# One encoder step: prompt attention with one subtracted map and one transpose, sample keys with four heads to a tile, and a pool of their own for the V rows

## The chip, the cores and the metric

The kernel runs on one core of a Trainium2 chip. The metric is the time of one launch in microseconds (us) on the device. Before the change it is 2169.43 us, the median of three runs (2169.18 to 2169.60).

## The reference, cut to what matters

One layer for 512 prompt tokens (one sequence) and 8 x 16 sample tokens (eight sequences, each with 1024 cached keys and values). Each of four attention heads makes two softmax maps and subtracts the second, times lam, from the first:

```python
def diff_core(q, k, v, qpos, kpos, lam):
    s = jnp.einsum('bqhmd,bkhmd->bhmqk', q, k, preferred_element_type=jnp.float32) * (B_DK ** -0.5)
    ...
    p = jax.nn.softmax(s, axis=-1)
    a = p[:, :, 0] - lam * p[:, :, 1]
    return jnp.einsum('bhqk,bkhd->bqhd', a.astype(v.dtype), v)

def run_group(x, c, past_k, past_v, ...):
    h = layer_norm(x) * (1 + scale1) + shift1
    p = h @ w_in[l]          # spatial gating, attention and gated DeltaNet read their columns
    ...
    y = jnp.concatenate([ya, yb, yc], axis=-1) @ w_out[l]
    x = layer_norm(DN_ALPHA * x + gate1 * y, ln1_g[l], ln1_b[l])
    h2 = layer_norm(x) * (1 + scale2) + shift2
    f = peer(h2, ...)        # 8 heads x top 16 of 16384 experts for each token
    x = layer_norm(DN_ALPHA * x + gate2 * f, ln2_g[l], ln2_b[l])

def peer_block(h, w_query, sub_keys, expert_u, expert_v):
    ...                      # ids (n, 128) and gates (n, 128) from two top-16 lists
    act = jax.nn.gelu(jnp.einsum('nkd,nd->nk', expert_u[ids], h))
    return jnp.einsum('nk,nkd->nd', (gates * act).astype(h.dtype), expert_v[ids])
```

## The kernel before

**The stages.** In order of time: the modulation and the combined projection; the attention stage, in which the prompt's attention, the samples' attention and the gated DeltaNet run side by side; the output projection; the choice of experts; the table; and the last stage, which works through all 16384 experts in 128 blocks of 128.

**The attention stage.** `lanes` (L127) writes four generators into one program: two chains of DeltaNet tiles (`gdn`), the prompt's attention (`attn_prompt` for the query tiles t = 0 to 3) and the samples' (`attn_sample`). A scheduler in the framework then orders the instructions of each engine at build time, and on the chip each engine runs its list in that order. `attn_prompt` takes a head at a time: two score products into PSUM, an addition of the mask with a row maximum on VectorE (DVE, L785), two exponentials on ScalarE (ACT, L789). The softmax's row factors and lam are then put on the diagonals of two 128x128 matrices `dg` (L794), and for each block of 128 keys two matrix products (s of map 0 by `dg` 0, plus s of map 1 by `dg` 1) give the transposed difference in PSUM: scaling, subtraction and transpose in one. `aT` (L801) is its copy, and a product with V follows. The DeltaNet ends before the prompt's lane; heads 1 to 3 of t = 3 stand alone behind it.

`attn_sample` takes one sequence b at a time. `fetch_k` loads its keys as eight tiles `ck` of one head and 512 positions (L1086, 256 KB, six buffers), `fetch_v` its values as four tiles `cv` (two buffers). `scores` multiplies: each head's product fills 32 of the 128 columns of TensorE (PE) and 32 rows of one PSUM bank, so that four heads make a bank of 512 positions. All loads are issued by SyncE (SP), whose queue is also in a fixed order.

**The table.** `table` (L1562) writes the gates into a dense table `gdense` in DRAM, expert by token: 12 chunks of four steps. A step makes one-hot tiles `ob`, `o1`, `o2` on DVE (L1585, L1588, L1589) and `o1a` on ACT, and PE multiplies them into PSUM (`sa`); ACT copies the result into `stg`, and each full `stg` (two buffers) is stored to `gdense` (L1596). The pool `tp` holds all of these; `o1`, `o1a` and `o2` have three buffers each.

**The last stage.** When `tx` closes, the pool `ep` takes over the table's memory. Each block m: load of 128 rows of U (`ur`) and of V (`vr`), split of each into a high and a low part (`uh`, `ul`, `vh`, `vl`), the table's columns (`gt`, one load for four blocks) times the activations of the block (`ga`, split into `wh`, `wl`), and products on PE. Eight blocks of activations have been made ahead (`LEAD`). Beside that GpSimd (POOL) gathers, row by row, the experts of the last prompt tile and of the samples (L1636), and DVE multiplies each gathered tile (L1645, L1651); the first of these multiplications needs `h2q`. This stage is written in the order in which it runs (`manual_schedule`).

Of the kernel before, what the change touches and what calls it, by code (L numbers as in the profile page):

```python
# [169 lines left out]
def body(tc, I, O):  # L170
# [4 lines left out]
    def T(pool, shape, tag, dt=F32, **kw):  # L175
        uid[0] += 1
        return pool.tile(list(shape), dt, tag=tag, name=f"{tag}_{uid[0]}", **kw)
# [20 lines left out]
    def C(name):  # L198
        a, b = COLS[name]
        return cst[:, a:b] if a < NC_ else mask[0][:, a - NC_:b - NC_]  # L200
# [570 lines left out]
    def attn_prompt(t, L):  # L771
# [6 lines left out]
        for h in range(4):  # L778
# [12 lines left out]
            V.tensor_tensor(out=sm[:, 1:2], in0=sm[:, 1:2], in1=nlam, op=ALU.mult)  # L791
            dg = T(gp, [P, 2, P], f"dg{L}")
            for m in range(2):
                V.tensor_scalar(out=dg[:, m, :], in0=ident, scalar1=sm[:, m:m + 1], scalar2=None, op0=ALU.mult)  # L794
            yield 0.43 * (t + 1)
            pa = bank()
            for c in range(t + 1):
                for m in range(2):
                    mm(pa[:, c * P:(c + 1) * P], s[:, m, c * P:(c + 1) * P], dg[:, m, :], m == 0, m == 1)
            aT = T(gp, [P, NP], f"aT{L}")  # L800
# [275 lines left out]
    def attn_sample():  # L1076
# [5 lines left out]
        def fetch_k(b):  # L1082
            for c in range(2):
                for h in range(4):
                    ck[b, h, c] = T(sp, [P, 512], "ck", bufs=6)
                    nc.sync.dma_start(out=ck[b, h, c], in_=I["ckT"][b, h, :, c * 512:c * 512 + 512])  # L1086

# [8 lines left out]
        def scores(b):  # L1096
# [6 lines left out]
            for c, (a, e) in enumerate(((0, 512), (512, 1024), (1024, NK))):  # L1103
                ps = sbank()
                for h in range(4):
                    ql = qbd[b % 2][:, h].rearrange("p m t -> p (m t)")
                    mm(ps[32 * h:32 * h + 32, 0:e - a], ql, ck[b, h, c] if c < 2 else kTs[:, h, b * TS:(b + 1) * TS])
                V.tensor_tensor_reduce(out=s[:, a:e], in0=ps[:, 0:e - a], in1=als[:, a:e], scale=1.0, scalar=NEG,
                                       op0=ALU.add, op1=ALU.max, accum_out=mx[:, c:c + 1])
# [440 lines left out]
    def gt_load(g):  # L1550
        gts[g] = T(ep, [P, 12, 4, 32], "gt2") if g % 2 else T(rw, [P, 12, 4, 32], "gt")
        nc.sync.dma_start(out=gts[g], in_=gd_[g])

    tx = ExitStack()
    tp = pool(tx, "tp", bufs=2, side="right")

    iob8 = T(tp, [P, P, 8], "iob8", BF16, bufs=1)
    V.tensor_copy(out=iob8, in_=C("iota").unsqueeze(2).to_broadcast([P, P, 8]))

    TOGETHER = 5  # L1560

    def table():  # L1562
        for t in range(3):
# [12 lines left out]
            for c in range(4):  # L1576
                stg = T(tp, [P, P, 32], "stg")
                for n0 in range(0, 32, 8):
                    col = 32 * c + n0
                    ob = T(tp, [P, P, 8], "ob", BF16, bufs=2)  # L1580
                    m = TOGETHER
                    o1 = T(tp, [P, P, m], "o1", bufs=3)
                    o1a = T(tp, [P, 8 - m, P], "o1a", bufs=3)
                    o2 = T(tp, [P, 8, P], "o2", bufs=3)
                    V.tensor_tensor(out=ob, in0=iob8, in1=i1b[:, col:col + 8].unsqueeze(1).to_broadcast([P, P, 8]), op=ALU.is_equal)  # L1585
# [4 lines left out]
                    for q in range(0, 8, 4):  # L1590
                        pg = bank("sa")
                        for n in range(q, q + 4):
# [4 lines left out]
                                  in_=stg.rearrange("p (g i) n -> p g (i n)", g=NG))  # L1597
                if (t, c) == (2, 2):
                    gts[0] = T(rw, [P, 12, 4, 32], "gt")
                    nc.sync.dma_start(out=gts[0][:, 0:11], in_=gd_[0, :, 0:11])  # L1600
# [12 lines left out]
    gs_q = gates[:, 3, :]  # L1613
    act_s, act_q = (T(ep, [P, P], n) for n in ("act_s", "act_q"))
    h2q = T(ep, [P, D], "h2q")
    nc.sync.dma_start(out=h2q, in_=h2qd)
    facc = {3: T(ac, [P, D], "acc", bufs=4), 4: T(rw, [P, D], "ycs")}
# [34 lines left out]

    vls, vs, ws, fin, fst = {}, {}, {}, {}, {}

    def v_load(n):
        vls[n] = T(ep, [P, D], "vr", bufs=3)
        nc.sync.dma_start(out=vls[n], in_=I["v"][n * P:(n + 1) * P, :])

    def v_hi(n):
        w = vls[n]  # L1660
        if n >= NBLK - LAST:
            V.tensor_tensor(out=w, in0=w, in1=fin["p"], op=ALU.mult)  # L1662
        vs[n] = (T(ep, [P, D], "vh", F32R, bufs=LAST), T(ep, [P, D], "vl", F32R, bufs=LAST))
        S.copy(out=vs[n][0], in_=w)  # L1664
# [4 lines left out]
    def g_hi(n):  # L1669
        ga = gas[n]  # L1670
        V.tensor_tensor(out=ga.rearrange("p (c n) -> p c n", c=12), in0=ga.rearrange("p (c n) -> p c n", c=12),  # L1671
                        in1=gts[n // 4][:, :, n % 4, :], op=ALU.mult)
        ws[n] = (T(ep, [P, ND], "wh", F32R, bufs=LAST), T(ep, [P, ND], "wl", F32R, bufs=LAST))
        S.copy(out=ws[n][0], in_=ga)  # L1674
# [49 lines left out]
    def final_gates():  # L1724
        gt2 = T(ep, [P, 2, D], "gates2")
        for k, (n, sm) in enumerate((("p", "selp"), ("s", "sels"))):
            fin[n] = gt2[:, k, :]
            for hf in range(2):
                pg = bank("mm")
                mm(pg, C(sm), gm[(5, hf)])  # L1730
                S.copy(out=fin[n][:, HALF[hf]], in_=pg)
# [13 lines left out]
    obanks = iter(["sa", "tp", "sa", "tp", "sa", "so"])  # L1745
    v_load(0)
    v_load(1)
    v_hi(0)
# [7 lines left out]
    for m in range(NBLK):  # L1756
# [5 lines left out]
        if m + 2 < NBLK:  # L1762
            v_load(m + 2)
        if m % 4 == 1 and m // 4 + 1 < NG:
            gt_load(m // 4 + 1)
# [72 lines left out]
```

## Time and profile before

| what | value |
|---|---|
| median of three runs | 2169.43 us (2169.18 to 2169.60) |
| the profiled execution | 2173.13 us |
| its span | 2171.4 us |
| PE busy | 1944.2 us (90%) |
| DVE busy | 1767.7 us (81%) |
| ACT busy | 701.9 us (32%) |
| POOL busy | 806.0 us (37%) |
| moved by DMA | 572.60 MB, mean 264 GB/s |

The span runs from the first to the last instruction of the profiled execution; the execution's own time is 1.7 us longer. An engine's busy time is the time in which at least one of its instructions ran. The attention stage stands at 268 to 538 us of the span, the table at 874 to 1018, the last stage from 1018 to the end.

### The profile page before, as it was taken

What the parts mean: (1) busy time and instruction counts of PE and PEld (TensorE: products, weight loads), DVE (VectorE), ACT (ScalarE), POOL (GpSimd) and SP (SyncE); (2) the same over time, 40 slices, a digit from 0 to 9 for tenths busy, and PEclk for the clock granted to TensorE, in tenths of its full rate; (3) what the DMA queues carried; (4) which work ended last, traced back from release to release, by engine and by line L of the source; (5) the groups of instructions that cost most, each with busy time, mean ns of one, the idle gap of its engine ahead of it and who ended that gap; (6) DMA issues with size and microseconds to landing.
All of it is one profiled execution on the core that took longest, in us unless ns stands there. A gap on an engine that the chain in (4) does not pass through costs nothing.

```text
span 2171.4 us, 32392 instructions
## 1 busy us (share of the span) xinstructions
PE 1944.2 (90%) x11971; PEld 1630.7 (75%) x11971; DVE 1767.7 (81%) x3939; ACT 701.9 (32%) x1241; POOL 806.0 (37%) x637
## 2 busy tenths in 40 slices
PE   5999999997996991897999999999999999999983
PEld 3888855675565881896898888888888888888862
DVE  5752146675788999985899999999999999999987
ACT  3331222332113320786433323333333333333320
POOL 2321222110004210100466666665666666556610
PEclk8999989998997995999999999999999999999996
DMA  7354365523333210567999999999999999999961
GB/s 288 117 183 167 105 224 172 183 83 117 117 132 134 95 40 0 175 183 210 352 405 405 399 388 394 398 399 398 395 404 404 405 404 396 395 380 404 398 233 68
DMA packets 203977, 572.60 MB, mean 264 GB/s; under 512 B 20863, under 2 KB 73599, under 8 KB 198954
## 3 DMA queue, kind: packets, MB, share of 16 engines
q1 hardware_dynamic: 121994, 293.43, 37.3%
q0 software_dynamic: 73728, 268.47, 31.5%
q10 hardware_dynamic: 8096, 8.63, 1.2%
q8 instruction: 94, 1.54, 0.3%
q14 instruction: 65, 0.53, 0.1%
HBM read 535.57 MB, written 34.36 MB: 262 GB/s over the span
## 4 chain that ended last, share of the span: by engine, by line
PE 34%; DVE 20%; POOL 18%; issue 18%; DMA 6%; ACT 3%; SPq 0%; POOLq 0%; ACTq 0%; DVEq 0%
PE mm L188 15%; POOL acc L1636 9%; POOL rows L1636 9%; PE sa L188 7%; PE a L188 5%; PE g L188 3%; DVE acc L1645 2%; DVE vl L1667 1%; DVE rows L1645 1%; ACT uh L243 1%; DMA acc<-in_v_dram,ids 1%; DVE ycs L1651 1%; DMA acc<-in_u_dram,idq 1%; DVE acc L1651 1%; PE ad L188 1%
## 5 line engine op out<-in xcount | busy, mean ns | idle before, releaser
L1674 ACT CAST wh<-ga 128x384 fp32r<-128x384 f32 x128 | 65.7, 514 | 693.6 <-DVE ga L1671 693.4
L188 PE MATMUL mm<-h2h,uh 128*128 128x384 f32 x1024 | 202.8, 339 | 10.2 <-ACT uh L243 8.9
L188 PEld LDWEIGHTS mm<-h2h,uh 128*128 128x128 f32 x1024 | 178.9, 188 | 32.4 <-ACT uh L243 24.8
L188 PE MATMUL mm<-h2h,ul 128*128 128x384 f32 x1024 | 198.3, 334 | 0.0
L188 PE MATMUL mm<-h2l,uh 128*128 128x384 f32 x1024 | 198.1, 334 | 0.0
L244 DVE TENSOR_TENSOR ul<-ur,uh 128x1024 fp32r<-128x1024 f32 x127 | 155.6, 1225 | 49.5 <-ACT uh L243 49.0
L1636 POOL DMA_INDIRECT acc<-in_u_dram,idq x65 | 83.4, 1283 | 281.0 <-DVE act_q L1645 202.2
L188 PE MATMUL sa<-vh,wh 128*128 128x512 f32 x384 | 153.1, 399 | 35.9 <-ACT wh L1674 31.0
L188 PE MATMUL sa<-vl,wh 128*128 128x512 f32 x384 | 160.8, 419 | 26.8 <-DVE vl L1667 26.8
L188 PEld LDWEIGHTS mm<-h2h,ul 128*128 128x128 f32 x1024 | 179.3, 188 | 0.0
L188 PEld LDWEIGHTS mm<-h2l,uh 128*128 128x128 f32 x1024 | 179.3, 188 | 0.0
L1667 DVE TENSOR_TENSOR vl<-vr,vh 128x1024 fp32r<-128x1024 f32 x128 | 156.3, 1221 | 13.0 <-DMA vr<-in_v_dram 13.0
L188 PE MATMUL sa<-vh,wl 128*128 128x512 f32 x384 | 152.0, 396 | 0.0
L1664 ACT CAST vh<-vr 128x1024 fp32r<-128x1024 f32 x128 | 133.3, 1041 | 38.0 <-DVE vr L1662 21.4
L243 ACT CAST uh<-ur 128x1024 fp32r<-128x1024 f32 x128 | 133.9, 1047 | 15.1 <-PE mm L188 15.1
L188 PE MATMUL sa<-o,o 128*128 128x128 f32 x480 | 118.6, 408 | 12.2 <-DVE o L1589 12.2
L188 PEld LDWEIGHTS sa<-vl,wh 128*128 128x128 f32 x384 | 73.2, 191 | 65.1 <-DVE vl L1667 52.0
L188 PEld LDWEIGHTS sa<-o,o 128*128 128x128 f32 x480 | 94.8, 207 | 20.9 <-DVE o L1589 12.6
L188 PEld LDWEIGHTS sa<-vh,wh 128*128 128x128 f32 x384 | 73.0, 190 | 49.4 <-ACT wh L1674 33.5
L244 POOL TENSOR_TENSOR wlo<-raw,whi 128x2048 fp32r<-128x2048 f32 (+1 forms) x12 | 55.7, 4640 | 141.5 <-ACT whi L243 122.4
L1636 POOL DMA_INDIRECT acc<-in_v_dram,ids x65 | 84.1, 1294 | 52.1 <-DVE ycs L1651 46.9
L188 PE MATMUL tp<-vh,wh 128*128 128x512 f32 x256 | 101.6, 397 | 0.0
(472 smaller groups left out, 4762.6 us busy)
## 6 DMA issues: line engine op xcount, KB each, us to landing
ur<-in_uT_dram SPq DMA_DIRECT2D x128, 512.0 KB, 6.7
vr<-in_v_dram SPq DMA_DIRECT2D x128, 512.0 KB, 6.6
raw<-in_wada_dram SPq DMA_DIRECT2D x24, 1024.0 KB, 6.7
gdense<-stg SPq DMA_DIRECT2D x12, 2048.0 KB, 8.7
gt<-gdense SPq DMA_DIRECT2D x31, 768.0 KB, 9.3
ck<-in_ckT_dram SPq DMA_DIRECT2D x64, 256.0 KB, 4.2
cv<-in_cv_dram SPq DMA_DIRECT2D x32, 512.0 KB, 4.1
wqr<-in_wq_dram SPq DMA_DIRECT2D x32, 512.0 KB, 3.2
```

The lines of the kernel that those rows point to most:

```text
L188: PE.matmul(out, lhsT=lhsT, rhs=rhs, start=start, stop=stop, **kw)
L243: S.copy(out=hi, in_=raw)
L244: e_lo.tensor_tensor(out=lo, in0=raw, in1=hi.bitcast(F32), op=ALU.subtract)
L1636: G.indirect_dma_start(out=r, out_offset=None, in_=I["v"] if k else I["u"], in_offset=bass.IndirectOffsetOnAxis(ap=who[t][0][:, s:s + 1], ...
L1645: V.tensor_tensor_reduce(out=r, in0=r, in1=h2, scale=1.0, scalar=0.0, op0=ALU.mult, op1=ALU.add, accum_out=act[:, s:s + 1])
L1651: V.scalar_tensor_tensor(out=facc[t], in0=r, scalar=act[:, s:s + 1], in1=facc[t], op0=ALU.mult, op1=ALU.add)
L1664: S.copy(out=vs[n][0], in_=w)
L1667: V.tensor_tensor(out=vs[n][1], in0=vls.pop(n), in1=vs[n][0].bitcast(F32), op=ALU.subtract)
L1674: S.copy(out=ws[n][0], in_=ga)
```

## The change

It has three parts. In `attn_prompt` the two `dg` matrices go: ACT scales map 0 by its row factor, DVE adds map 1 times its own (which holds minus lam), both in place in `s`, and PE makes a plain transpose of each block of 128 keys. In `attn_sample` a key tile holds four heads and 256 positions (512 KB, three buffers), and each head's product covers 256 positions. For the last stage the V rows get a pool `ev`, opened ahead of the table's, their first two loads stand in the table, `o1`, `o1a` and `o2` have two buffers each, and the tiles of `ep` are allocated in another order, with the second `gt` load ahead of `h2q`.

```diff
-            dg = T(gp, [P, 2, P], f"dg{L}")
-            for m in range(2):
-                V.tensor_scalar(out=dg[:, m, :], in0=ident, scalar1=sm[:, m:m + 1], scalar2=None, op0=ALU.mult)
+
+            S.activation(s[:, 0, 0:n], s[:, 0, 0:n], AF.Copy, scale=sm[:, 0:1])
+            V.scalar_tensor_tensor(out=s[:, 0, 0:n], in0=s[:, 1, 0:n], scalar=sm[:, 1:2], in1=s[:, 0, 0:n], op0=ALU.mult, op1=ALU.add)
             yield 0.43 * (t + 1)
             pa = bank()
             for c in range(t + 1):
-                for m in range(2):
-                    mm(pa[:, c * P:(c + 1) * P], s[:, m, c * P:(c + 1) * P], dg[:, m, :], m == 0, m == 1)
+                transpose(pa[:, c * P:(c + 1) * P], s[:, 0, c * P:(c + 1) * P])
...
         def fetch_k(b):
-            for c in range(2):
-                for h in range(4):
-                    ck[b, h, c] = T(sp, [P, 512], "ck", bufs=6)
-                    nc.sync.dma_start(out=ck[b, h, c], in_=I["ckT"][b, h, :, c * 512:c * 512 + 512])
+            for c in range(4):
+                ck[b, c] = T(sp, [P, 4, 256], "ck", bufs=3)
+                nc.sync.dma_start(out=ck[b, c], in_=I["ckT"][b, :, :, c * 256:c * 256 + 256].rearrange("h d k -> d h k"))
...
-                for h in range(4):
-                    ql = qbd[b % 2][:, h].rearrange("p m t -> p (m t)")
-                    mm(ps[32 * h:32 * h + 32, 0:e - a], ql, ck[b, h, c] if c < 2 else kTs[:, h, b * TS:(b + 1) * TS])
+                for q in range(2 if c < 2 else 1):
+                    for h in range(4):
+                        ql = qbd[b % 2][:, h].rearrange("p m t -> p (m t)")
+                        if c < 2:
+                            mm(ps[32 * h:32 * h + 32, 256 * q:256 * q + 256], ql, ck[b, 2 * c + q][:, h, :])
+                        else:
+                            mm(ps[32 * h:32 * h + 32, 0:TS], ql, kTs[:, h, b * TS:(b + 1) * TS])
...
+    ev = pool(es, "ev")
     tx = ExitStack()
     tp = pool(tx, "tp", bufs=2, side="right")
...
+    vls = {}
+
+    def v_load(n):
+        vls[n] = T(ev, [P, D], "vr", bufs=3)
+        nc.sync.dma_start(out=vls[n], in_=I["v"][n * P:(n + 1) * P, :])
...
-                    o1 = T(tp, [P, P, m], "o1", bufs=3)
-                    o1a = T(tp, [P, 8 - m, P], "o1a", bufs=3)
-                    o2 = T(tp, [P, 8, P], "o2", bufs=3)
+                    o1 = T(tp, [P, P, m], "o1", bufs=2)
+                    o1a = T(tp, [P, 8 - m, P], "o1a", bufs=2)
+                    o2 = T(tp, [P, 8, P], "o2", bufs=2)
...
                 if (t, c) == (2, 2):
+                    v_load(0)
+                    v_load(1)
                     gts[0] = T(rw, [P, 12, 4, 32], "gt")
...
     act_s, act_q = (T(ep, [P, P], n) for n in ("act_s", "act_q"))
+
+    def w_pair():
+        return T(ep, [P, ND], "wh", F32R, bufs=LAST), T(ep, [P, ND], "wl", F32R, bufs=LAST)
+
+
+    first_w = w_pair()
+    first_vh = T(ep, [P, D], "vh", F32R, bufs=LAST)
     h2q = T(ep, [P, D], "h2q")
+    gates2 = T(ep, [P, 2, D], "gates2")
+    gt_load(1)
+    first_vl = T(ep, [P, D], "vl", F32R, bufs=LAST)
     nc.sync.dma_start(out=h2q, in_=h2qd)
...
-    v_load(0)
-    v_load(1)
     v_hi(0)
...
-        if m % 4 == 1 and m // 4 + 1 < NG:
+        if m % 4 == 1 and 1 < m // 4 + 1 < NG:
             gt_load(m // 4 + 1)
```

`v_hi` and `g_hi` use the first tiles for block 0, and `final_gates` uses `gates2`; nothing else is in the diff.

What the build makes of it: outside the attention stage the lists of PE, DVE, ACT and POOL hold the same instructions in the same order as before. Two places show what moved.

In PE's list of the attention stage, the key products of the sample sequence b = 3 (tiles `ck`; `cv` and `vnk` are values of b = 2, `vt` and `kT` belong to the prompt's lane, `g` to the DeltaNet), before:

```order
L188 MATMUL a_571_3620<-ck_3306,qbd_2566 32x512
L188 MATMUL a_553_3529<-cv_3269,aT_3420 32x128 x8
L188 MATMUL a_560_3589<-vt_1985,aT_556_3577 128x128 x2
L188 MATMUL a_571_3620<-ck_3308,qbd_2566 32x512
L188 MATMUL a_571_3620<-ck_3310,qbd_2566 32x512
L188 MATMUL a_571_3620<-ck_3312,qbd_2566 32x512
L188 MATMUL a_588_3666<-kT_1598,qT_2304 128x256
L188 MATMUL a_553_3529<-cv_3271,aT_3420 32x128 x8
L188 MATMUL a_553_3529<-vnk_3273,aT_3420 32x128 x4
L188 MATMUL a_572_3626<-ck_3314,qbd_2566 32x512
```

and after the change:

```order
L188 MATMUL a_550_3601<-ck_3300,qbd_2566 32x256 x4
L188 MATMUL a_550_3601<-ck_3302,qbd_2566 32x256 x4
L188 MATMUL g_567_3680<-h_498_3340,S_391_2880 64x64
L188 MATMUL a_539_3570<-vt_1985,aT_535_3558 128x128
L188 MATMUL a_532_3512<-cv_3255,aT_3404 32x128 x8
L188 MATMUL a_539_3570<-vt_1985,aT_535_3558 128x128
L188 MATMUL a_551_3611<-ck_3304,qbd_2566 32x256 x4
L188 MATMUL a_563_3647<-kT_1598,qT_2304 128x256
L188 MATMUL a_532_3512<-cv_3257,aT_3404 32x128 x8
L188 MATMUL a_532_3512<-vnk_3259,aT_3404 32x128 x4
L188 MATMUL a_564_3650<-kT_1598,qT_2304 128x256
L188 MATMUL a_551_3611<-ck_3306,qbd_2566 32x256 x4
```

Before, a sequence's first head stood alone and three heads followed together, and so in the second half. Now the four heads of a quarter follow each other; of the 32 quarters of the eight sequences six are cut into one and three.

In SP's list, from the last store of the table on, before:

```order
L1596 DMA gdense_8727<-stg_9749 128x32x128
L1616 DMA h2q_9846<-h2qd_5857 128x1024
L1657 DMA vr_9860<-in_v_dram 128x1024
L1657 DMA vr_9862<-in_v_dram 128x1024
L1497 DMA ur_9879<-in_uT_dram 128x1024
L1657 DMA vr_9881<-in_v_dram 128x1024
L1497 DMA ur_9945<-in_uT_dram 128x1024
L1657 DMA vr_9947<-in_v_dram 128x1024
L1552 DMA gt_2021_9949<-gdense_8727 128x1536
```

and after the change, first at the table's start, then from its last chunk on:

```order
L1499 DMA ur_9829<-in_uT_dram 128x1024
L1567 DMA vr_9694<-in_v_dram 128x1024
L1567 DMA vr_9696<-in_v_dram 128x1024
L1567 DMA vr_9831<-in_v_dram 128x1024
L1499 DMA ur_9895<-in_uT_dram 128x1024
L1605 DMA gdense_8671<-stg_8688 128x32x128
```

```order
L1611 DMA gt_9698<-gdense_8671 128x1408
L1605 DMA gdense_8671<-stg_9700 128x32x128
L1554 DMA gt_1947_9802<-gdense_8671 128x1536
L1637 DMA h2q_9800<-h2qd_5801 128x1024
L1567 DMA vr_9897<-in_v_dram 128x1024
L1499 DMA ur_9963<-in_uT_dram 128x1024
```

Three V tiles and two U tiles moved from behind the table's last store to ahead of its first; the second `gt` load moved ahead of `h2q`, and waits for the last store. In the built program the cast of the first V tile (`vh` of block 0) waits for the store before the last, and that of the second (`vh` of block 1) for the last, because their buffers lie over the two `stg` tiles.

## Rows read from the trace of the kernel before

**Rows 1.** Windows, all engines: stretch, us; busy us of PE, PEld, DVE, ACT, POOL; clock; DMA; GB/s

```profile
278.00:475.00 197.00, 186.87 (x2489) 123.65 (x2488) 118.23 (x456) 61.70 (x181) 37.65 (x56) 0.98 0.52 170
475.00:503.40 28.40, 25.74 (x360) 19.17 (x354) 22.66 (x100) 7.92 (x22) 2.19 (x3) 0.98 0.11 40
503.40:538.20 34.80, 23.85 (x100) 17.46 (x99) 15.18 (x64) 8.53 (x19) 0.00 (x0) 0.77 0.30 108
1010.00:1014.00 4.00, 4.00 (x22) 3.68 (x21) 1.50 (x2) 3.04 (x8) 0.00 (x0) 1.00 1.01 290
1034.00:1900.00 866.00, 839.95 (x4148) 739.52 (x4149) 818.46 (x1073) 282.13 (x405) 530.08 (x420) 1.00 1.01 396
```

**Rows 2.** Windows of tile ck alone: stretch, us; busy us of PE and PEld

```profile
278.00:475.00 197.00, 38.06 (x128) 5.30 (x128) 0.98 0.52 170
```

**Rows 3.** Windows of tile dg alone: PE, PEld and DVE

```profile
278.00:475.00 197.00, 15.49 (x96) 12.06 (x96) 7.89 (x24) 0.98 0.52 170
475.00:503.40 28.40, 2.05 (x16) 1.86 (x16) 1.11 (x4) 0.98 0.11 40
503.40:538.20 34.80, 10.54 (x48) 9.93 (x48) 0.95 (x4) 0.77 0.30 108
```

**Rows 4.** Timeline of PE: start us, duration us, line, out<-in, shape

```profile
430.47 1.04 PE L188 MATMUL a<-ck,qbd 128*32 128x512 f32 x2
445.85 1.07 PE L188 MATMUL a<-ck,qbd 128*32 128x512 f32 x8
...
553.42 1.04 PE L205 MATMUL tp<-cst,acc 128*128 128x128 f32 x8
```

**Rows 5.** Timeline of PE: work that stands between two key quarters

```profile
351.60 0.71 PE L188 MATMUL a<-vt,aT 128*128 128x128 f32 x4
353.23 0.70 PE L188 MATMUL a<-kT,qT 64*128 64x256 f32 x2
368.84 1.08 PE L188 MATMUL a<-cv,aT 128*32 128x128 f32 x32
```

**Rows 6.** Tile ck's loads, and PE's waits for them from 278 to 475

```profile
DMA to landing us min/median/max: 2.7/4.2/8.5
```

```profile
PE a L188 <- DMA ck<-in_ckT_dram: 1.5, 2, 0.9
```

**Rows 7.** Timeline: a PE transpose, ACT and DVE steps; last, the page's costliest groups

```profile
276.03 1.09 PE L205 MATMUL g<-cst,qkv 128*128 128x128 f32 x4 [1.59 <-DVE qkv L861]
482.72 0.28 DVE L794 TENSOR_SCALAR dg<-cst,sm 128x128 f32<-128x128 f32 x1
498.41 0.72 ACT L789 ACTIVATE s<-s,mx 128x512 f32<-128x512 f32 x1
```

```profile
L1667 DVE TENSOR_TENSOR vl<-vr,vh 128x1024 fp32r<-128x1024 f32 x128 | 156.3, 1221 | 13.0 <-DMA vr<-in_v_dram 13.0
```

**Rows 8.** Timeline of the last two steps of the table

```profile
1009.55 1.22 DVE L1588 TENSOR_TENSOR o<-cst,slots 128x1024 f32<-128x1024 f32 x1
...
1010.69 0.82 DVE L1589 TENSOR_TENSOR o<-ob,slots 128x640 f32<-128x640 bf16 x1
...
1012.00 0.59 ACT L1594 COPY stg<-sa 128x512 f32<-128x512 f32 x1
...
1014.78 2.47 PE L188 MATMUL sa<-o,o 128*128 128x128 f32 x10
```

**Rows 9.** Timeline from the table's last store to the first gathered tile

```profile
1018.56 0.36 SPq L1596 DMA_DIRECT2D gdense<-stg  x1
...
1033.93 1.04 ACT L1664 CAST vh<-vr 128x1024 fp32r<-128x1024 f32 x1
...
1043.05 1.22 DVE L1645 CUSTOM_DVE_ANT_0 acc<-acc,h2q 128x1024 f32<-128x1024 f32 x1
```

**Rows 10.** DMA issues from 1000 to 1045: count, KB each, median us to landing

```profile
gdense<-stg SPq DMA_DIRECT2D x2, 2048.0 KB, 9.4
...
h2q<-h2qd SPq DMA_DIRECT2D x1, 512.0 KB, 10.3
```

More of the change, by code (lines that the diff above doesn't have):

```diff
@@ L1651, in consume @@
             V.scalar_tensor_tensor(out=facc[t], in0=r, scalar=act[:, s:s + 1], in1=facc[t], op0=ALU.mult, op1=ALU.add)
[L1653 to L1657, printed above, removed]
+    vs, ws, fin, fst = {}, {}, {}, {}
     def v_hi(n):
@@ L1662, in v_hi @@
             V.tensor_tensor(out=w, in0=w, in1=fin["p"], op=ALU.mult)
-        vs[n] = (T(ep, [P, D], "vh", F32R, bufs=LAST), T(ep, [P, D], "vl", F32R, bufs=LAST))
+        vs[n] = (T(ep, [P, D], "vh", F32R, bufs=LAST), T(ep, [P, D], "vl", F32R, bufs=LAST)) if n else (first_vh, first_vl)
         S.copy(out=vs[n][0], in_=w)
@@ L1672, in g_hi @@
                         in1=gts[n // 4][:, :, n % 4, :], op=ALU.mult)
-        ws[n] = (T(ep, [P, ND], "wh", F32R, bufs=LAST), T(ep, [P, ND], "wl", F32R, bufs=LAST))
+        ws[n] = w_pair() if n else first_w
         S.copy(out=ws[n][0], in_=ga)
@@ L1724, in final_gates @@
     def final_gates():
-        gt2 = T(ep, [P, 2, D], "gates2")
         for k, (n, sm) in enumerate((("p", "selp"), ("s", "sels"))):
-            fin[n] = gt2[:, k, :]
+            fin[n] = gates2[:, k, :]
             for hf in range(2):
```

## The prediction

> **What bounds the kernel now.** I read the busy times by stage first. From 278 to 475 us, in the attention stage, PE works 186.87 of 197 us while DVE works 118 and DMA stands at 0.52; from 475 to 503.4 PE works 25.74 of 28.4 [rows 1]. In both the granted clock is 0.98, practically the upper of PE's two levels. So up to 503.4 PE is the bound: 212.6 busy us of 225.4, 12.8 idle. A microsecond of PE work saved there is a microsecond of time, unless a new wait takes its place. From 503.4 to 538.2 PE is busy 23.85 of 34.8 us at a clock of 0.77: a chain of three heads, one behind the other, in which each engine waits for the next. There the length of the chain counts. The table is a PE stage too (4.00 of 4 us), and in the last stage PE (839.95 of 866), DVE (818.46) and DMA (1.01 at 396 GB/s) are all nearly full. The diff touches none of the last stage's loop, so I let that stage keep its length and only move its start.
>
> **Part 1, sample keys.** Before, the products on `ck` take 38.06 us of PE up to 475 [rows 2]. One product alone (x2, two records each) takes 1.04 us, and four heads together (x8) 1.07 [rows 4]: the four use different columns and run side by side, so a lone head costs as much as four. 38.06 / 1.055 is 36 passes, where eight sequences with two halves and four heads each need 16; the cut into one and three pays twice. After, there are 32 quarters with half the positions, six of them cut in two: 38 passes. Does half the length take half the time? The products on `cv` say so: x32 with 128 positions take 1.08 us [rows 5], as x8 with 512 do, so small pieces cost nothing extra. I take 0.55 a pass: 20.9 us, a gain of **17.2** (17.7 at exactly half; a loss of 2.6 if a pass stayed at 1.07).
>
> **Part 1, what it may cost.** Three buffers hold three of a sequence's four quarters; the fourth's load can only be issued when PE has left the first. Between the first and the fourth stand, by the order, two quarters (1.1 us), two V tiles of the sample before (1.08), its new V (0.27), a product of the prompt (0.36 to 0.71) and a score pair or two (0.70 each) [rows 5]: some 4 to 4.6 us, against a landing of 4.2 us median, 2.7 to 8.5, in the trace of before [rows 6]. PE waited for `ck` just two times then, 1.5 us in all [rows 6]. A key tile now comes in pieces of 1 KB a row, before 2 KB. Near the table's end, with stores of 512 B pieces, DMA is full at 290 GB/s, in the last stage, with 4 KB rows, at 396 [rows 1]. For 512 KB these are 1.8 and 1.3 us, so I add 0.5 to the landing. That gives about 0.75 us of wait for each of eight sequences: **6 us** back. Bounds: nothing (the landing at 4.2 just fits), and 33 us if each of the eight lands at 8.5 (some 4.1 late). I stay near the lower, since the median is what eight loads meet, and DMA is half idle.
>
> The Trainium skill, "DMA: Bandwidth & Descriptors", section Specifications, puts the smallest piece that reaches line rate at 512 B. By it the 1 KB pieces would cost nothing and the 6 us would be about 2; the 290 GB/s row does not agree with it, though that stretch is mostly stores.
>
> **Part 2, prompt maps.** The products on `dg` take 15.49 + 2.05 us of PE before 503.4, for 112 records, that is 56 products [rows 3]. After, 28 transposes stay. A transposition of 128 x 128 on PE takes 1.04 us for x8 in the trace, at full clock [rows 4]: 0.13 each, 3.6 us. Gain **13.9**. What DVE and ACT get in exchange (one pass over up to 512 columns each; the two `dg`, 0.28 us each, go [rows 7]) lies beside PE, as both engines have over 40% idle there [rows 1]. Were that cover gone, 10 heads at about 0.8 us would cost 8.
>
> Up to 503.4 that makes 17.2 + 13.9 - 6 = **25 us**.
>
> In the tail, 48 records on `dg` take 10.54 us [rows 3]; after it 12 transposes take 1.6 at full clock, 3.3 at the 1.09 us for x4 seen at the low one [rows 7]: 7.3 to 8.9 less. On the chain stand now an ACT pass of 512 columns (0.72, as the exponential [rows 7]) and a DVE pass of 512, for which half of the 1221 ns for 1024 stands, 0.61 [rows 7], in place of two `dg` steps of together 0.56: +0.8 a head. The first of the three heads overlaps its predecessor, so two count: +1.6. Net 5.7 to 7.3 less; I take **6**. Bounds: 7.5, and nothing if with less work PE falls to the low clock for the whole tail: the 13 us of other products stand at 0.77, and at 0.5 would take up to 6.5 more.
>
> **Part 3, the table with two buffers.** PE sets its step: one starts at 1014.78 [rows 8], and the step two before has ended at 1012.00, where ACT copies its result. With three buffers `o2` of that step was made at 1009.55, ahead of that; with two it must wait for 1012.0. Then `o2` and `o1`, started 1.14 apart [rows 8], are done 1.14 + 0.82 = 2.0 later, at 1014.0, 0.8 before PE needs them. ACT is busy 3.04 of 4 us there [rows 1], 2.3 us a step of 2.97, and would be done at 1014.3, 0.5 ahead. So **0**, with a thin lead. If it is missed by 1 us a step, 46 steps cost 46 us.
>
> **Part 3, the start of the last stage.** Now the last store is issued at 1018.56, and the V rows come only behind it and behind `h2q`: `vh` of block 1 is cast at 1033.93 and the first gathered tile multiplied at 1043.05 [rows 9]. After, the V rows lie ready. Block 0's `vh` waits for the store before the last, and block 1's for the last one, whose landing takes 9.4 us [rows 10]: 1018.56 + 9.4 = 1028.0. That is 6.0 us ahead of 1033.93, and the chain behind it (`wh`, `uh`, the first `acc`) comes to 1037.1. On SP the second `gt` load waits for the same landing, and `h2q` stands behind it: issued at about 1028.4, it has 8.7 us until 1037.1; before it took 10.3 with five loads around it, which are gone [rows 10]. So it may be up to 1.6 late for DVE, while POOL's gathers go on. The last stage is full on DMA and PE, so its start is what counts, and the five loads of 512 KB moved into the table (2.5 MB, 6.3 us at 396 GB/s [rows 1]) agree in size. Gain **6**, from 3 (if `h2q` is late and what it feeds decides) to 8. Such moves also change where POOL's gathers meet the loads; no row prices that.
>
> **Sum.** 25 + 6 + 6 = 37. The profiled execution is 2173.1 us; it becomes 2136. It stands 3.7 above the median of the runs, so on that scale 2132.4: **2132 us**, 1.7% less.
>
> **The rivals.**
> - *A late fourth quarter.* PE's time saved is spent waiting for the key tile that is loaded too late. For it: three buffers, a short gap, a landing of up to 8.5 [rows 6]. Against it: the median and the idle half of DMA. With all eight late, 33 us of wait in place of 6: 2132 + 27 = **2159**; half of it gives 2146.
> - *The halved products do not shrink*: 38 passes at 1.07, 2.6 more in place of 17.2 less, **2152**. Against it: `cv` [rows 5].  The Trainium skill, "TensorEngine Tiling (Array Packing)", section Key Properties, says that a change of the tiling drains the engine; a fixed cost for each change would act in this direction, but rows 4 and 5 show none of a size that matters.
> - *The boundary gives nothing*: the last stage is bound by POOL's gathers or DMA, and an earlier V gains nothing; **2138**.
> - *The tail at the low clock*: shorter work in the tail is eaten by the clock; **2138**.
> - *Slower: the table becomes bound by its buffers.* PE must wait in each step because `o2`, `o1` or `o1a` come after PE's release. For it: the lead is 0.5 to 0.8 us of 2.97. It decides from the point at which the pair and its semaphores take over 2.8 us after the release (ACT 2.5 of work now). At 1 us a step: 2132 + 46 = **2178**.
>
> **How the numbers follow.** Forecast 54%, late quarter 15%, no shrinking 4%, boundary 12%, low clock 8%, table 7%. The lower end adds the favourable bounds: no added wait (6), the tail's and the boundary's best (1.5 and 2), a full halving and transposes a little shorter (1 to 2): 2121. The upper end takes in the late quarter nearly whole: 2159. Outside lie the table's 7%, a part of the late quarters and some 5% below. About 0.2%, 4.3 us, is what a measurement of this kernel can tell from no change: only a late quarter together with a weak boundary or tail comes that near (4%), so faster 89%, within 4%, slower 7%.
>
> **What would show it.** After, the windows of `ck` on PE should add to about 21 us, those of the transposes to `pa` to 3.6 before the tail and some 2 to 3 in it; the attention stage should end some 31 us earlier with PE's idle time before the tail near 19 us. PE's waits for `ck` should be some 6 us. The table's step should stay at 2.97 us. `vh` of block 1 should follow the last store's landing, and the first `acc` the last store's issue by 18.5 us instead of 24.5. I am wrong if PE's idle time in the attention stage grows by over 15 us, if the table's 144 us grow, or if the last stage, from its first product to the end, changes by more than 2 us.

## The result, and the profile after

The changed kernel takes 2143.2 us, the kernel before 2169.5 beside it, both as medians: 26 us less. The ratio of the means is 0.9874 (95% interval 0.9844 to 0.9905). The forecast was 2132, with a range of 2121 to 2159.

The profiled execution after is 2143.5 us long, 0.3 above the median; that of before stood 3.7 above its own. Its span is 29.7 us shorter than that of before, and the difference comes from these stretches. Their marks are the last copy of V in the combined projection (L559), the start of the DeltaNet's last product, the first product of the output projection, the first product of the table, and the issue of its last store.

| stretch | before, us | after, us | difference | forecast |
|---|---|---|---|---|
| start to the last copy of V | 232.3 | 234.0 | +1.7 | 0 |
| to the DeltaNet's last product | 270.9 | 249.4 | -21.5 | -25 |
| the tail, to the output projection | 35.3 | 32.6 | -2.7 | -6 |
| to the table | 336.0 | 335.9 | -0.1 | 0 |
| the table | 144.1 | 144.0 | -0.1 | 0 |
| last store to the end | 1152.8 | 1145.8 | -7.0 | -6 |

The two stretches of the attention stage as windows, with the columns of [rows 1], before:

```profile
232.30:503.20 270.90, 251.54 (x3132) 179.57 (x3126) 153.16 (x609) 78.12 (x220) 50.77 (x69) 0.97 0.44 144
503.20:538.50 35.30, 24.35 (x106) 17.85 (x103) 15.63 (x66) 8.53 (x19) 0.00 (x0) 0.77 0.30 108
```

and after:

```profile
234.00:483.40 249.40, 225.03 (x3176) 169.36 (x3176) 152.62 (x595) 83.76 (x234) 51.14 (x69) 0.96 0.48 157
483.40:516.00 32.60, 19.91 (x70) 12.31 (x67) 16.11 (x64) 9.97 (x21) 0.00 (x0) 0.69 0.33 115
```

Ahead of the tail PE works 26.5 us less, and its idle time grows from 19.4 to 24.4 us. The lines that answer to [rows 2, 3] are, in the groups of PE's instructions from 234.0 to 483.4 us (busy us, mean ns | idle before, releaser):

```profile
L188 PE MATMUL a<-ck,qbd 128*32 128x256 f32 x256 | 22.9, 403 | 0.1
L205 PE MATMUL a<-cst,s 128*128 128x128 f32 x28 | 6.1, 307 | 2.3 <-DVE s L794 2.2
```

The key products fall from 38.06 to 22.9 us, and the transposes take 6.1 us where the products on `dg` took 17.54. PE's longest waits there (us in total, times, longest):

```profile
PE g L188 <- DMA mask<-in_mask_dram: 4.8, 1, 4.8
PE a L188 <- DMA cv<-in_cv_dram: 3.1, 5, 1.0
PE a L205 <- DVE s L794: 2.2, 2, 1.2
PE g L188 <- DVE rs_s L1116: 1.8, 2, 1.1
```

and, of the same list before the change, three that are compared below:

```profile
PE a L188 <- DVE cb L1118: 1.6, 1, 1.6
PE a L188 <- DMA ck<-in_ckT_dram: 1.5, 2, 0.9
PE a L188 <- DMA cv<-in_cv_dram: 1.0, 1, 1.0
```

The mask wait was there before (4.6 us). A wait of PE for `ck` is no longer in the list. The tail is read in the timeline of its second head (start us, duration us; idle before in brackets), first before:

```profile
512.89 0.19 ACT L789 ACTIVATION_READ_ACCUMULATOR s<-s,mx 128x1 f32 x1
...
513.39 0.48 DVE L794 TENSOR_SCALAR dg<-cst,sm 128x128 f32<-128x128 f32 x2
...
513.82 3.75 PE L188 MATMUL a<-dg,s 128*128 128x128 f32 x16 [3.90 <-DVE dg L794]
...
518.30 2.08 PE L188 MATMUL a<-vt,aT 128*128 128x128 f32 x8 [0.73 <-ACT aT L801]
...
530.60 1.16 PE L188 MATMUL a<-vt,aT 128*128 128x128 f32 x8 [0.73 <-ACT aT L801]
```

(the last line is the product with V of the third head) and after:

```profile
492.69 0.18 ACT L789 ACTIVATION_READ_ACCUMULATOR s<-s,mx 128x1 f32 x1
...
493.14 0.16 DVE L790 RECIPROCAL sm<-sm 128x2 f32<-128x2 f32 x1
...
493.33 0.72 ACT L793 ACTIVATE s<-s,sm 128x512 f32<-128x512 f32 x1 [0.46 <-DVE sm L790]
...
494.08 0.75 DVE L794 SCALAR_TENSOR_TENSOR s<-s,sm 128x512 f32<-128x512 f32 x1 [0.26 <-ACT s L793]
...
494.89 1.12 PE L205 MATMUL a<-cst,s 128*128 128x128 f32 x4 [4.97 <-DVE s L794]
...
496.68 2.08 PE L188 MATMUL a<-vt,aT 128*128 128x128 f32 x8 [0.68 <-ACT aT L800]
```

From the end of the last exponential (492.87) to the transposes there are 2.02 us; before, the same step, from 513.08 to 513.82, took 0.74. The table's end and the start of the last stage, which answer to [rows 8, 9]:

```profile
989.38 1.23 DVE L1597 TENSOR_TENSOR o<-cst,slots 128x1024 f32<-128x1024 f32 x1 [0.41 <-PE sa L188]
...
990.52 0.82 DVE L1598 TENSOR_TENSOR o<-ob,slots 128x640 f32<-128x640 bf16 x1
...
992.15 2.47 PE L188 MATMUL sa<-o,o 128*128 128x128 f32 x10
...
995.94 0.36 SPq L1605 DMA_DIRECT2D gdense<-stg  x1
...
1004.67 1.05 ACT L1681 CAST vh<-vr 128x1024 fp32r<-128x1024 f32 x1 [5.55 <-DMA gdense<-stg]
...
1013.56 1.22 DVE L1666 CUSTOM_DVE_ANT_0 acc<-acc,h2q 128x1024 f32<-128x1024 f32 x1
```

`o2` now waits for PE and the pair is done at 991.34, 0.81 us before PE starts: the lead that was worked out (0.8). The second `vh` waits for the last store, and the first gathered tile is multiplied (by `h2q`, the last line) 17.6 us after that store's issue, where it was 24.5.

### The profile page after: what moved, and what is told of

Its sections match the earlier page's. It is cut to its first block, busy times and chain, and to the rows that moved or that the text cites. A ratio compares the mean times of both kernels' runs of the same rounds, so it can differ in the third digit from the quotient of the medians.

```text
span 2141.7 us, 32339 instructions
## 1 busy us (share of the span) xinstructions
PE 1918.2 (90%) x11979; PEld 1615.7 (75%) x11979; DVE 1767.3 (83%) x3923; ACT 707.8 (33%) x1257; POOL 806.1 (38%) x637
## 4 chain that ended last, share of the span: by engine, by line
PE 31%; POOL 21%; issue 19%; DVE 18%; DMA 6%; ACT 3%; ACTq 0%; POOLq 0%; SPq 0%; DVEq 0%
PE mm L188 15%; POOL acc L1657 10%; POOL rows L1657 10%; PE sa L188 7%; PE a L188 4%; PE g L188 2%; DVE ycs L1672 2%; PE ad L188 1%; DVE vl L1684 1%; DMA acc<-in_v_dram,ids 1%; ACT uh L243 1%; DMA rows<-in_v_dram,ids 1%; DMA cv<-in_cv_dram 1%; PE tp L188 1%; DVE rows L1666 1%
## 5 line engine op out<-in xcount | busy, mean ns | idle before, releaser
L188 PE MATMUL sa<-vl,wh 128*128 128x512 f32 x384 | 161.8, 421 | 26.7 <-DVE vl L1684 26.5
L188 PE MATMUL sa<-o,o 128*128 128x128 f32 x480 | 118.6, 408 | 12.2 <-DVE o L1598 12.2
L1657 POOL DMA_INDIRECT rows<-in_u_dram,ids x65 | 82.8, 1275 | 54.3 <-DVE act_s L1666 49.4
L188 PE MATMUL tp<-vl,wh 128*128 128x512 f32 x256 | 101.8, 398 | 0.0
```

Of the source, the lines that this page charges most:

```text
L188: PE.matmul(out, lhsT=lhsT, rhs=rhs, start=start, stop=stop, **kw)
L1657: G.indirect_dma_start(out=r, out_offset=None, in_=I["v"] if k else I["u"], in_offset=bass.IndirectOffsetOnAxis(ap=who[t][0][:, s:s + 1], ...
```

## The experiments

Each ratio is of the means, to the kernel before on the same chip, whose median was 2172.4 us for e1 to e4, 2175.5 for e5 to e8 and 2171.4 for e9 to e12.

An edit of the attention stage changes more than its own instructions, since the framework's scheduler orders the lists of the stage anew. In e1 and e2 about a tenth of PE's instructions and a sixth of DVE's that both kernels share stand at another place of the order than before, and in e11 as many or more against the changed kernel. What this order does to the time by itself was not tested.

**e1, the sample keys alone.**

```diff
-            for c in range(2):
-                for h in range(4):
-                    ck[b, h, c] = T(sp, [P, 512], "ck", bufs=6)
+            for c in range(4):
+                ck[b, c] = T(sp, [P, 4, 256], "ck", bufs=3)
```

> The kernel before with the sample keys' edit alone (tiles of four heads and 256 positions). Theory: in the attention stage a saved microsecond of PE counts, so the 15 us less on the key products in the trace after the change show at the end, less some 3 to 5 us of new waits: 9 to 13 us faster (2156 to 2160), and the tail behind the DeltaNet keeps its 35 us. Rival 1, the waits of late loads eat the gain: 0 to 4 us. Rival 2, the two attention edits need each other: under 6 us alone.

2158.4 us, 0.9936 (0.9915 to 0.9956): 14 us less. The stretch before the tail:

```profile
235.90:491.10 255.20, 231.26 (x3260) 178.01 (x3257) 152.28 (x609) 77.07 (x220) 51.13 (x69) 0.98 0.47 153
```

15.7 us shorter than before, and the gain at the end is a little above the theory; the tail is 33.9. Both rivals fall: late loads do not eat the gain, and the edit does not need the other. PE works 20.3 us less, though the key products give only 15 of them: the DeltaNet's products, the same in both kernels, take 100.8 us instead of 106.5. So busy time of unchanged work moves with its surroundings, and PE's idle time grew here too, from 19.4 to 23.9 us.

**e2 and e10, the prompt maps alone**, twice.

```diff
-            dg = T(gp, [P, 2, P], f"dg{L}")
...
+            S.activation(s[:, 0, 0:n], s[:, 0, 0:n], AF.Copy, scale=sm[:, 0:1])
+            V.scalar_tensor_tensor(out=s[:, 0, 0:n], in0=s[:, 1, 0:n], scalar=sm[:, 1:2], in1=s[:, 0, 0:n], op0=ALU.mult, op1=ALU.add)
```

> The kernel before with the prompt maps' edit alone (scale, subtract, one transpose). Theory: 11 us less of PE before the tail (17.5 of products against 6.1 of transposes in the trace after) and 2.7 us in the tail, no new loads: 12 to 15 us faster (2154 to 2158). Rival, DVE and ACT, which get a pass each, hold the heads back: the tail becomes longer and no more than 8 us are left.

> The prompt maps' edit alone, measured again. Theory: its gain alone is well under the 12 to 15 us first expected, since 16 us of PE work less meet 9 us more of waits in the trace; 4 to 8 us faster than the kernel before. Rival 1: it gains nothing by itself (within 2 us). Rival 2: the first measurement was disturbed, and it gains 10 us and more.

2170.4 us, 0.9992 (0.9974 to 1.0009), and 2169.9 us, 0.9991 (0.9978 to 1.0003): 2 us less, and at most 6 by the intervals. The first expectation, 12 to 15, is refuted, and so is its repetition's second rival. The 4 to 8 us of the repetition are missed as well, though its interval reaches 4.8; its first rival, no gain, fits. The rival of e2 had the size right and the place wrong, since the tail does not become longer. The stretch before the tail of e10, and some of PE's waits in it:

```profile
234.50:502.60 268.10, 243.02 (x3048) 170.99 (x3047) 152.53 (x593) 84.86 (x234) 49.45 (x69) 0.95 0.43 146
```

```profile
PE a L188 <- DVE cb L1117: 3.6, 4, 2.2
PE a L205 <- DVE s L794: 3.2, 2, 2.4
PE g L205 <- DVE grs L859: 2.2, 1, 2.2
```

PE works 8.5 us less than before (12.2 in e2), but the stretch is only 2.8 us shorter (4.3 in e2): idle time grew by 5.7 us (7.9 in e2). e3 leaves this stage as it was before and has 268.3 us there; against it the edit gains 0.2 and 1.7. The waits for DVE on `cb` (1.6 us before), on the subtracted map `s` and on `grs` hold most of the new idle time. `cb` and `grs` belong to the samples and the DeltaNet, which the edit touches only by the new order; in the changed kernel the wait for `cb` is 1.0 us. Whether these waits come from the order or would be there in any is not shown. The tail is 2 to 2.5 us shorter. Whether the end gains these 5 to 7 us or only 2 stays open: from the last store to the end e2's profile has 1148.4 us and e10's 1156.1, with the same instructions.

**e3, the V rows' pool and the table's two buffers alone.**

```diff
+    ev = pool(es, "ev")
...
-                    o1 = T(tp, [P, P, m], "o1", bufs=3)
+                    o1 = T(tp, [P, P, m], "o1", bufs=2)
...
+                    v_load(0)
+                    v_load(1)
```

> The kernel before with the V rows' pool and the table with two buffers alone. Theory: table unchanged at 144 us, the first gathered multiplication 17 to 18 us behind the issue of the last store instead of 24.5, the end 6 to 8 us earlier (2161 to 2163). Rival, the boundary's gain is noise of two profiles or is given back in the last stage: 0 to 3 us.

2164.7 us, 0.9971 (0.9951 to 0.9990): 6 to 8 us less. The table takes 144.1 us, the first gathered multiplication comes 17.6 us after the last store, and the end 1146.0 us after it, before 1152.8. As the theory has it. Nor is it an accident of two profiles: from the last store to the end the five profiles with the old boundary (before, e1, e2, e4, e10) have 1148.4 to 1156.1 us, the seven with that of the change (the changed kernel, e3, e5, e6, e7, e9, e11) 1139.2 to 1146.0.

**e4, keys and maps together**, without the pool.

> Both attention edits, boundary as before. Theory: the sum of the two runs before it within 3 us, some 20 to 24 us faster (2145 to 2149). Rival, both gain the same idle time or the shorter stage runs into a common limit (DVE, the loads): at least 5 us less than the sum.

2151.5 us, 0.9897 (0.9863 to 0.9931): 21 to 22 us less. The sum of e1 and e2 is 16, outside the theory's 3 us, on the other side than the rival: on top of the keys the maps' edit is worth more. The intervals (7 us each way for e4) allow a plain sum too, so the surplus is not shown. With e3's share of 6 to 8 us the changed kernel's gain is complete.

**e9, the changed kernel again.**

> The changed kernel once more, on one chip with the three runs beside it. Theory: 24 to 29 us faster than the kernel before, as in its first measurement (ratio 0.987). A second profile tells how much one program's attention stage varies between profiles: some 5 us, if what e4 and the changed kernel differ by is no effect of the boundary. Rival: the V pool shortens the attention stage too, and the stage comes out at the first profile's 282 us again, not at 287.

2143.0 us, 0.9865 (0.9842 to 0.9887): 28 us less, as expected. The stretch before the tail, and the same stretch in e8, e4 and e6:

```profile
235.90:486.80 250.90, 226.46 (x3174) 170.30 (x3170) 152.20 (x592) 83.87 (x234) 50.69 (x69) 0.95 0.47 156
```

```profile
235.50:483.20 247.70, 223.78 (x3176) 168.10 (x3172) 152.20 (x592) 83.67 (x234) 50.70 (x69) 0.96 0.49 158
235.40:489.90 254.50, 228.83 (x3176) 171.79 (x3176) 153.27 (x595) 83.72 (x234) 51.21 (x69) 0.94 0.46 154
234.10:490.40 256.30, 230.32 (x3176) 174.06 (x3172) 153.27 (x595) 83.94 (x234) 50.92 (x69) 0.94 0.47 153
```

With this, the stretch is known from five profiles in which PE, DVE and ACT have the same instructions in the same order there: 247.7 (e8), 249.4, 250.9, 254.5 (e4) and 256.3 (e6). It varies by 8.6 us, and it is the longer the lower the granted clock of TensorE is: 0.96, 0.96, 0.95, 0.94 and 0.94. Which of the two brings the other about is not shown. The rival, by which the V pool shortens the stage, falls: e6 has the pool and the longest stretch. From the last store to the end the kernel's two profiles have 1145.8 and 1142.0 us.

**e11, key products made twice.**

```diff
+                            for _ in range(2):
                                 mm(ps[32 * h:32 * h + 32, 256 * q:256 * q + 256], ql, ck[b, 2 * c + q][:, h, :])
```

> The changed kernel with each sample key product made twice into the same place: 22 us more of PE work before the tail, nothing else. Theory, PE's work counts in full there: the stage before the tail grows by 18 to 22 us. Rival, by now waits share the bound, and work that comes back is partly taken up by them: 8 to 14 us, and PE's idle time before the tail falls by as much as is missing.

2153.4 us, 0.9920 (0.9894 to 0.9945). The stretch before the tail, all of PE and tile `ck` alone (columns as in [rows 2]):

```profile
234.60:494.20 259.60, 238.65 (x3432) 180.13 (x3432) 154.04 (x595) 84.65 (x234) 51.19 (x69) 0.96 0.46 151
```

```profile
234.60:494.20 259.60, 42.05 (x512) 19.05 (x512) 0.96 0.46 151
```

The key products grow by 19.2 us, the stretch by 8.7 against e9 and by 10.2 and 11.9 against the two profiles with the same granted clock, 0.96 (the changed kernel's first and e8); by the medians the end comes 10 us later. The theory's 18 to 22 is refuted, and the size is the rival's: added here, a microsecond of key products costs about half a microsecond. Its reason holds in part only. Against e9 PE's idle time falls from 24.4 to 21.0, a third of what is missing; the larger part is that the other products take 7.0 us less, the DeltaNet's 100.9 us instead of 104.1.

**e5, the row factor applied late.**

```diff
-            S.activation(s[:, 0, 0:n], s[:, 0, 0:n], AF.Copy, scale=sm[:, 0:1])
...
-            S.copy(out=osb[:, h * P:(h + 1) * P], in_=po[:, 0:P])
+            S.activation(osb[:, h * P:(h + 1) * P], po[:, 0:P], AF.Copy, scale=rr[:, 0:1])
```

> The changed kernel, with the scaling of map 0 by ACT taken out: DVE adds map 1 times the ratio of the two row factors, and the row factor itself is applied where ACT copies the product with V out of PSUM. Theory: in the tail the step from the last exponential to the transpose (2.0 us in the changed kernel, 0.7 before the change) is on the path twice to three times, so 0.8 to 0.9 us a head go: the tail shortens from 32.4 to about 30 us, the end comes 1.5 to 3 us earlier than the changed kernel's 2143. Rival: DVE, not ACT, holds the heads in the tail, and the tail stays at 32 us.

2137.5 us, 0.9839 (0.9821 to 0.9857). The tail:

```profile
482.80:513.50 30.70, 20.78 (x69) 12.39 (x65) 15.32 (x61) 8.18 (x18) 0.00 (x0) 0.55 0.37 125
```

1.9 us shorter than in the changed kernel, so the ACT pass was on the path. The end gains more than the tail, but the intervals of this ratio and of e9's overlap.

**e6, work for PE in the tail's waits.**

```diff
+            if t == 3 and h > 1:
+                pf = T(pb, [P, 512], "a1", bufs=2)
+                for _ in range(3):
+                    mm(pf, aT[:, 0:P], alp[:, 0, :])
```

> The changed kernel, with three products of 128 x 512 that nobody reads, put on PE behind the score products of heads 2 and 3 of the last prompt tile, where PE waits some 5 us for the softmax. Theory: the products with V take 2.08 us in the tail, after such a wait, because the granted clock is at the lower level; with PE kept at work the granted clock of the tail rises from 0.69 to above 0.9, two V products take about 1.2 us each and the score pair behind the first 1.6 instead of 2.0, and the tail shortens by 1.5 to 2.5 us. Rival: the length of the V products has another cause (the copy ahead of them, the weights); they stay at 2.08 us, and the added products lengthen the tail by 0 to 2 us.

2143.3 us, 0.9851 (0.9823 to 0.9879). The tail, and PE's timeline of its second head:

```profile
490.40:521.80 31.40, 24.66 (x83) 13.60 (x80) 15.84 (x63) 9.97 (x21) 0.00 (x0) 0.79 0.34 121
```

```profile
496.77 2.84 PE L188 MATMUL a<-alp,aT 128*128 128x512 f32 x6
501.88 0.66 PE L205 MATMUL a<-cst,s 128*128 128x128 f32 x4 [2.27 <-DVE s L794]
503.22 1.87 PE L188 MATMUL a<-vt,aT 128*128 128x128 f32 x8 [0.68 <-ACT aT L804]
505.02 2.24 PE L188 MATMUL a<-kT,qT 64*128 64x512 f32 x4
```

The granted clock rises from 0.69 to 0.79, not above 0.9. The transposes fall from 1.12 to 0.66 us, the V products only from 2.08 to 1.87 (1.72 for the last head), and the tail by 1.2. Windows over the transposes of the second head and the V products of the second and third tell why:

```profile
501.88:502.55 0.67, 0.66 (x4) 0.42 (x4) 0.00 (x0) 0.00 (x0) 0.00 (x0) 1.00 0.00 0
503.22:505.02 1.80, 1.80 (x8) 1.57 (x8) 0.00 (x0) 0.00 (x0) 0.00 (x0) 0.57 0.00 0
513.29:514.80 1.51, 1.51 (x9) 1.51 (x9) 0.00 (x0) 0.00 (x0) 0.00 (x0) 0.64 1.02 404
```

The granted clock is 1.00 over the transposes, but 0.57 and 0.64 over the V products. In the changed kernel it is 0.50 over both, and over the V products that take 1.16 us in the kernel before it is 1.00. So the clock does lengthen this chain, and the rival falls; the added products keep the clock up for the transposes and not for the V products, and the tail gains less than the theory had. The end gains nothing that the measurement shows.

**e7, the next head's scores ahead.**

```diff
-        for h in range(4):
+        def maps(h):
...
+        for h in range(4):
+            s, sm = nxt
+            if h < 3:
+                nxt = maps(h + 1)
+                yield 0.43 * (t + 1)
```

> The changed kernel, with the scores of the next head written ahead of the transposes of this one, so that the softmax of a head overlaps the products of another. Theory: what is left in the tail is a chain of waits, not work; one head less stands in it in full, the PE work of it moves beside the DeltaNet, and the stretch from the DeltaNet's last product to the output projection falls from 32.4 to some 20 us, of which PE's 7 us of moved work come back before: 4 to 8 us faster than the changed kernel. Rival: the stretch before the tail is bound by PE and by its waits alike, and gets as much longer as the tail gets shorter: 0 to 2 us.

2129.2 us, 0.9796 (0.9780 to 0.9813): 14 us less than the changed kernel by the medians, 15 to 17 by the ratios, and more than expected.

```profile
234.00:488.00 254.00, 231.04 (x3198) 172.43 (x3200) 153.62 (x605) 86.58 (x242) 51.81 (x69) 0.95 0.49 157
488.00:504.60 16.60, 10.71 (x50) 6.68 (x45) 12.28 (x53) 6.28 (x13) 0.00 (x0) 0.79 0.51 174
```

The tail is halved, from 32.6 to 16.6 us, and the stretch before it takes over that work for some 3 to 5 us: what stood in the tail were mostly waits. Together the two stretches are 11 to 13 us shorter than in the changed kernel's two profiles. The rest of this profile's gain lies behind the last store (1139.2 us), in code that the edit leaves alone.

**e8, the first V tiles off the last store's memory.**

```diff
+    pre_w = {0: w_pair(0), 1: w_pair(1)}
+    pre_vh = {0: v_hi_tile(0), 1: v_hi_tile(1)}
+    gates2 = T(ep, [P, 2, D], "gates2")
...
     nc.sync.dma_start(out=h2q, in_=h2qd)
+    gt2_first = T(ep, [P, 12, 4, 32], "gt2")
```

> The changed kernel, with the tiles of the last stage laid out so that the first two blocks' V and weight tiles lie over the store before the last, not over the last one, and the load of h2q issued ahead of the second table load. Theory: the wait for the last store's landing (8.7 us after its issue) goes from the head of the last stage; the first gathered multiplication comes some 11 to 13 us after that issue instead of 17.6, and the end 3 to 6 us earlier than the changed kernel's. Rival: the transfers decide (the store, then all loads and gathers at full share): the multiplication comes earlier, but the end by under 1.5 us.

2140.0 us, 0.9848 (0.9831 to 0.9864).

```profile
995.66 0.36 SPq L1605 DMA_DIRECT2D gdense<-stg  x1
...
1009.12 1.22 DVE L1674 CUSTOM_DVE_ANT_0 acc<-acc,h2q 128x1024 f32<-128x1024 f32 x1
```

The multiplication comes 13.5 us after the store instead of 17.6. The end lies 1141.4 us after it, 4.4 below the first profile of the changed kernel and 0.6 below e9's. That is inside what one program varies by; not settled by this run.

**e12, e5, e7 and e8 together.**

> The changed kernel with the next head's scores ahead, the row factor at the eviction, and the early V tiles together. Theory: the three act at different places (14 to 19 us, 2 to 4 us and 2 to 4 us in the runs by themselves), the first two share the tail, so some 17 to 22 us less than the changed kernel, 0.977 to 0.979 of the kernel before. Rival: what the boundary gains is given back in the last stage, and the row factor is covered once heads overlap: no more than heads ahead alone (14 us, 0.980).

2128.3 us, 0.9813 (0.9785 to 0.9840): the rival, though the interval just reaches the theory's upper edge. The tail is 16.0 us, 0.6 less than in e7, and from the last store to the end there are 1139.0 us, as in e7 (1139.2), though the first gathered multiplication comes 13.6 us after the store instead of 17.5. So the early V tiles show no gain that lasts, in a stretch that varies by 7 us among profiles of one boundary, and the row factor is covered once the heads overlap. The heads ahead alone (e7) are the version to keep: 14 us below the changed kernel by the medians, 0.9796 against 0.9865 and 0.9874 by the ratios.

## Why the prediction was right or wrong

The sign and the range held, and the first part is the largest, as forecast. 11 us are missing: 2143 for 2132. Of them 3.7 are the offset between the profile of before and its median, which was taken off and which the profile after hardly has (0.3); 1.7 lie ahead of the attention stage, in code that did not change; the rest, 3.5 and 3.3 less 1.0, are terms.

**Sample keys, 17.2 us: right in kind, 15.2 measured.** The halved products do shrink: 22.9 us for 38 passes, 0.60 each where 0.55 was taken. The difference shows in a quarter alone and two in a row, after:

```profile
299.65 0.64 PE L188 MATMUL a<-ck,qbd 128*32 128x256 f32 x8
...
341.20 1.07 PE L188 MATMUL a<-ck,qbd 128*32 128x256 f32 x16
```

A second quarter behind its like adds 0.43, so 0.2 us stand once for each group of quarters, and half the length is not half the time of a group. What of this is the price of a change of tiling is not told apart. Alone, the edit brought 14 us.

**The late fourth quarter, 6 us: wrong place, and the size right by luck.** PE's idle time grew by 5.0 us, but its waits for `ck` fell from 1.5 to 0.1 (1.2 in e8, with the same instructions in the stage). What is longer is the wait for the samples' V rows (`cv`, 1.0 before, 3.1 after), and waits for DVE, of which 2.2 on `s` come from the other edit, to which the prediction gave no wait. The Trainium skill, "DMA: Bandwidth & Descriptors", section Specifications, by which pieces of 1 KB cost nothing, came nearer to the waits for `ck` than the 0.5 us taken from the stores' rate; the landing time itself shows in no row after. (The gap between the first and the fourth quarter is 3.5 to 4.6 us by the prediction's own pieces, not 4 to 4.6.)

**Prompt maps, 13.9 us: the term that failed.** Its work was over-priced, and its worth by itself too. Transposes take 6.1 us, not 3.6: the 0.13 each came from eight in a row [rows 4], while here they stand by one to four between other products (0.22 each). So PE is relieved of 11.4 us. But the sentence that "a microsecond of PE work saved there is a microsecond of time, unless a new wait takes its place" was used without asking of each edit which wait stands behind it. In e2 and e10 the stretch gains 2.8 to 4.3 us, with 5.7 to 7.9 us of new idle time, and e11 gets back about half of what it adds. It is no fixed rate: in e1 15 us less of key products gave 15.7 of stretch, and on top of the keys the maps' edit is worth 7 us at the end (e4 against e1), where alone it is worth 2. So the 94% at which PE was busy [rows 1] did not tell what a saved microsecond is worth. What decides it in each order of the lists stays open.

**The tail, 6 us: 2.7.** The products on `dg` went as priced (10.54 to 3.35 us, 7.2 less). The chain ahead of the transposes grew by 1.28 us a head, not 0.8: DVE's pass takes 0.75 where 0.61 was taken from the row of 1024 columns, and two hand-overs between engines were not counted. And part of the rival of the low clock came true: the V products take 2.08 us each for three heads, 6.2 us, where they took 4.4 before, and the granted clock fell from 0.77 to 0.69. e6 shows that work for PE in the waits takes part of this back. (The rival's bound of 6.5 us is a little low by its own numbers: 13.3 us of products at 0.77 take 7 more at 0.5.)

**The table, 0: right**, as is its reason, the lead of 0.8 us. The step's products are as before (118.6 us for 480, mean 408 ns). **The boundary, 6: 7.0**, by the chain described: the store lands in 8.7 us instead of 9.4, the second `vh` follows it, and the last stage from the first gathered multiplication on keeps its length (1128.4 and 1128.1 us; over all profiles it lies between 1122 and 1132, so that the two agree so closely is luck). (The five loads that moved are 2.6 MB, 6.6 us at 396 GB/s, not 6.3; the term did not rest on it.) e3 gives this part by itself. Against the last store PE's first product comes 12 us earlier, and gains nothing by it, since it then waits for the chain. With that, one of the prediction's signs of being wrong came up: from its first product to the end the last stage grew from 1137.3 to 1142.5 us, more than the 2 us allowed. The sign named the wrong mark: the stage moves with its first gathered multiplication, not with PE's first product.

## What to carry to other kernels

- A busy share of 94% does not make every microsecond of an engine's work count. Ask for each edit what its neighbours wait for once the engine is free sooner, and run each edit alone: here one gave its work back in full, the other nearly nothing. Doubling one kind of work (e11) measures the rate for that kind in that order, here a half.
- Where heads or tiles stand one behind another at the end of a stage, look for the chain of waits before shortening its pieces: letting the next one start ahead brought 14 us, the shorter pieces 2 to 3.
- Take the price of a short instruction from rows where it stands alone, as it will, not from a row of eight in sequence.

## What the runs showed of the hardware that was not expected

- The same instructions in the same order took 247.7 to 256.3 us before the tail (e8, the changed kernel, e9, e4, e6), and the granted clock fell from 0.96 to 0.94 in that order. Two profiles of one program differ by 8 us from the last store to the end (e2 and e10: 1148.4 and 1156.1). A sum made against one profile carries this with it.
- In the tail, where PE waits some 5 us for the softmax of each head, the granted clock is 0.69, and 0.79 with three products that nobody reads put into each of two waits. Four transposes then take 0.66 us, not 1.12, at a granted clock of 1.00, but the V products behind the next short wait only fall from 2.08 to 1.87 and 1.72, at 0.57 and 0.64.
